# A hybrid DeltaNet and neighbourhood-attention layer on one core: transposes issued thirteen steps later, output-projection loads ahead of the network's, one more product between the token halves

## The chip, the cores and the metric

The kernel runs on one core of a Trainium2 chip. The metric is the device time of one execution in microseconds (us), as the median of repeated runs. A profile of one execution goes with it: its span runs from the first instruction to the last, and every instruction, wait and transfer in it has a place on that axis. Places such as "at 266 us" below are on that axis.

## The reference

One layer acts on 1024 latent tokens of width 1024, with 256 context tokens beside them. All arithmetic is in 32-bit floating point.

```python
px = modulate(rms_norm(x, norm1_w[i]), sh1, sc1) @ w_in[i]
pc = modulate(rms_norm(ctx, norm1_w[i]), csh1, csc1) @ w_in[i]
dn_c, s_ctx_f, s_ctx_b = gated_deltanet(pc[..., :DN_IN], ...)      # 4 heads of 128, forward and backward scan
dn_x, _, _ = gated_deltanet(px[..., :DN_IN], ..., s_ctx_f, s_ctx_b)
na_x = neighborhood_attention(qx, kx, vx, kc, vc, na_rpb[i], rows) # 8 heads of 64
x = x + g1 * (jnp.concatenate([dn_x, na_x], axis=-1) @ w_out[i])
x = x + g2 * swiglu(modulate(rms_norm(x, norm2_w[i]), sh2, sc2), w_ffn_in[i], w_ffn_out[i])
```

The delta rule is computed in chunks. Each chunk needs the inverse of a unit triangular matrix of its keys. The feed-forward network (`swiglu`) multiplies by a 1024 x 5632 matrix (gate and up halves) and then by a 2816 x 1024 matrix.

## The kernel before, in words

**How products are made.** Every large operand is split into a rounded upper part and a remainder (`whi`/`wlo`, `uhi`/`ulo` for weights, `hh`/`hl`, `hB`/`lB`, `hT`/`lT` for activations). ACT makes the upper part with a cast, DVE or POOL the lower part with a subtraction, and PE runs three products: upper by upper, upper by lower, lower by upper. So one 128 x 128 block of weights against 512 tokens is three matmuls of 128x512.

**The input projection (to about 550 us).** A list `jobs` of weight blocks is worked through in order: two key blocks first, then keys, the value columns, the attention's keys and queries, the DeltaNet's queries, values and gates. A job over the latent tokens has eight steps (one for each 128 rows of the input width) with six matmuls of 512 columns each. Background work is written as generators, and a call of `bg.step(n)` after each step takes it on by `n` `yield`s: one to a step before the job numbered `turn` (14), two on the ten pieces of a `Wide` job, three to a step from `turn` on. The background queue holds `block_inverses` and behind it `preps`. It starts with job 5.

`block_inverses` makes the decay tables, puts 32 x 32 blocks into a layout `N` of 80 partitions with PE transposes (L902-905), inverts them with 30 rounds of two DVE operations (L913, L915), writes the diagonal (L918, a memset), and takes them back with 32 PE transposes into PSUM and eight ACT copies into `WK` (L921-926). Then come for each scan direction a DVE transpose (L932), a store to `x_d` (L934), a DVE product (L935) and another store (L937). `preps` follows: for each chunk it loads `kk`, `xc` (from `x_d`) and `e`, copies blocks on ACT and POOL, takes exponentials on ACT, multiplies on DVE (`kk`, L981) and runs small matmuls into a bank `pr`, with ACT (L991) and DVE (L999) copies between them. The four context chunks come first; the sixteen latent ones wait until the DeltaNet's queries are done (end of job 18). A generator of `preps` has seven steps for each chunk, three chunks in turn.

**The output projection (about 780 to 877 us).** `two_blocks` has begun the first two of eight output blocks on the attention half of the rows. After the scans, `up = Stream()` issues the first eight loads (256 KB each) of the network's weights (`wq`, L1382) on the SP queue. Then come the remaining halves of the weights of blocks 0 and 1 (`wraw`, L215, two buffers), two loads of `x`, and while block 0 finishes, the load of block 2's weights. Blocks 2 to 5 take all tokens at a time; from block 2 on PSUM banks come from a pool `psf`, opened when the pool of the scans is closed. The last two blocks are run by token half `t`. After each half, `finish(t)` adds the two blocks to `x2` (L1454), squares them on ACT (L1459) and sums the squares in `acc` (L1460), and `normed(t)` multiplies `acc` by ones on PE and takes logarithm and exponential on ACT into `rs` (L1443-1445).

**The network's first two blocks, `PLAIN = 2` (about 877 to 928 us).** `x2` is cut into four quadrants: `B11`, `B21` (rows of the width, first token half) and `B12`, `B22` (second half). `quadrant` turns each of its four slices into network input: scale on DVE (L1541), bias on ACT (L1542), cast on ACT (L1534), remainder on DVE (L1535). Eight calls of `product` of 24 matmuls each follow: for block `f`, half `t`, row half `i`. `up.next()` hands out split weights (six buffers), `up.ahead` makes more. `sums` (L1553) prepares combined quadrants T1 to T4 for the blocks that follow, which use a seven-product scheme of Strassen's kind. From there on the network runs to the end.

**Who sets the order.** Each engine and the SP queue run their instructions in a fixed order. It is made when the program is built: the framework goes through the code in order, holds ready instructions by priority of that order, and places each by a model of how long everything takes, so that an instruction can come ahead of an earlier one that the model thinks is not ready. `tc.keep_in_program_order` pins an instruction to the code's order among those that are pinned on its engine. A pool opened with `reuse_waits="tile"`, as `pools` does, waits for the tiles that held its memory before; a pool opened without it waits for the whole pool.

Of the kernel before, what the change touches and what calls it, by code (L numbers as in the profile page):

```python
# [9 lines left out]
F32 = mybir.dt.float32  # L10
# [20 lines left out]
PLAIN = 2  # L31
SEGS = [(0, 256), (256, 512), (768, 512)]
# [55 lines left out]
def hybrid(ctx, tc, a, dbg):  # L88
# [304 lines left out]
    with ExitStack() as bs:  # L393
# [459 lines left out]
        def block_inverses():  # L853
            with ExitStack() as gs:
# [64 lines left out]
                yield  # L919
# [527 lines left out]
    with ExitStack() as os_:  # L1447
# [3 lines left out]

        def add(b, s, p):

            dve.scalar_tensor_tensor(x2[:, b, s], p, modp[:, 16 + b:17 + b], x2[:, b, s], op0=OP.mult, op1=OP.add)  # L1454
# [3 lines left out]
            sq = uw.tile([128, 4, 128], F32, name="ws", tag="ws", bufs=3).rearrange("p a b -> p (a b)")  # L1458
            act.activation(sq, x2[:, b, s], AF.Square)  # L1459
            dve.tensor_tensor(acc[:, s], acc[:, s], sq, OP.add)  # L1460
# [3 lines left out]
        for b, (w, outs) in enumerate(zip(ws, begun)):  # L1464
# [37 lines left out]
        for t, s in enumerate(HV):  # L1502
            outs = [bank(), bank()]
            last.append(outs)
            for k in range(KT):
# [4 lines left out]
                if t == 1 and k == 2:  # L1510
                    normed(0)
            if t == 0:
                finish(0)
# [5 lines left out]
    with ExitStack() as us:  # L1519
# [16 lines left out]

        def quadrant(n):
            i, j = int(n[1]) - 1, int(n[2]) - 1
            for k in range(4):
                kk, t = 4 * i + k, B[n][:, k]  # L1540
                dve.scalar_tensor_tensor(t, t, w2s[:, kk:kk + 1], rs[:, HV[j]], op0=OP.mult, op1=OP.mult)  # L1541
                act.activation(t, t, AF.Identity, bias=modp[:, 24 + kk:25 + kk])  # L1542
                split(X[n], B[n], k)
# [38 lines left out]
        quadrant("B11")  # L1582
        finish(1)
        quadrant("B21")
        prev = out_tiles(0)
        for f in range(PLAIN):
            po = [[bank(), bank()] for _ in range(2)]
            g = prev[f]
            w = [up.next(), None]
            for t in range(2):  # L1590
                for i in range(2):
                    if f == 0 and t == 1 and i == 0:
                        for n in ("B12", "B22"):
                            quadrant(n)
                    if t == 0 and i == 1:
# [187 lines left out]
```

## Time and profile before

| | |
|---|---|
| median of 3 runs | 1526.71 us (1526.71 to 1532.21) |
| the profiled execution | 1526.16 us |
| its span | 1524.4 us, mean granted clock 0.992 |
| PE busy | 1460.5 us (96%) |
| DVE, ACT, POOL busy | 66%, 47%, 12% of the span |
| share of the 16 DMA engines taken by the SP queue | 55.7%, 274 MB |

A row of the timeline gives start, duration, engine, line, operation, output and inputs, shapes and count of merged instructions, and in brackets how long the engine had been idle before and what ended that. PEld is the load of weights, which overlaps PE. SPq rows are the issue of transfers. A row of the windows gives the stretch, its length, the busy time of PE, PEld, DVE, ACT and POOL with the count of instructions, the granted clock of PE as a share of full speed, the share of the DMA engines and GB/s. A row of the waits gives who waited for whom, the total in us, how many times, and the longest.

### The profile page before, as it was taken

What the parts mean: (1) busy time and instruction counts of PE and PEld (TensorE: products, weight loads), DVE (VectorE), ACT (ScalarE), POOL (GpSimd) and SP (SyncE); (2) the same over time, 40 slices, a digit from 0 to 9 for tenths busy, and PEclk for the clock granted to TensorE, in tenths of its full rate; (3) what the DMA queues carried; (4) which work ended last, traced back from release to release, by engine and by line L of the source; (5) the groups of instructions that cost most, each with busy time, mean ns of one, the idle gap of its engine ahead of it and who ended that gap; (6) DMA issues with size and microseconds to landing.
All of it is one profiled execution on the core that took longest, in us unless ns stands there. A gap on an engine that the chain in (4) does not pass through costs nothing.

```text
span 1524.4 us, 23483 instructions
## 1 busy us (share of the span) xinstructions
PE 1460.5 (96%) x8365; PEld 1206.5 (79%) x8365; DVE 1004.4 (66%) x1898; ACT 710.6 (47%) x1387; POOL 184.8 (12%) x253
## 2 busy tenths in 40 slices
PE   5999998999999999998899989999999999999998
PEld 3789787778877778887787878888888888888887
DVE  4787579354677427779986388765655556599642
ACT  5443362683366546566642374333333334354441
POOL 0154610342134300000100000000000000000000
PEclk9999999899999999999999999999999999999999
DMA  9377223654477789998539315333233335798742
GB/s 367 112 229 238 61 78 122 234 152 168 132 217 253 223 280 278 285 273 237 164 102 330 109 35 186 111 104 104 104 104 103 104 104 173 246 364 294 235 152 83
DMA packets 209830, 276.29 MB, mean 181 GB/s; under 512 B 15968, under 2 KB 116912, under 8 KB 208688
## 3 DMA queue, kind: packets, MB, share of 16 engines
q1 hardware_dynamic: 208992, 274.41, 55.7%
q8 instruction: 66, 1.08, 0.3%
q14 instruction: 52, 0.43, 0.1%
q10 hardware_dynamic: 720, 0.37, 0.1%
HBM read 209.93 MB, written 68.98 MB: 183 GB/s over the span
## 4 chain that ended last, share of the span: by engine, by line
PE 75%; DVE 11%; DMA 4%; issue 4%; ACT 4%; POOL 1%; SPq 0%; POOLq 0%; DVEq 0%; ACTq 0%
PE ps L98 50%; PE blk L98 12%; PE sc L98 4%; PE pr L98 3%; PE m L98 3%; PE sc L102 2%; DVE tt L913 2%; DVE N L915 2%; DVE cacc L471 1%; PE m L102 1%; PE pm L98 1%; ACT bt L340 1%; DVE bt L337 1%; DMA wad<-wa 1%; DMA wraw<-w_out 1%
## 5 line engine op out<-in xcount | busy, mean ns | idle before, releaser
L98 PE MATMUL ps<-hT,uhi 128*128 128x512 f32 x496 | 147.1, 391 | 3.1 <-ACT hT L1534 3.1
L98 PE MATMUL ps<-lT,uhi 128*128 128x512 f32 x496 | 146.3, 389 | 0.0
L98 PE MATMUL ps<-hT,ulo 128*128 128x512 f32 x496 | 146.2, 389 | 0.0
L98 PE MATMUL blk<-hh,whi 128*128 128x512 f32 (+1 forms) x456 | 139.5, 398 | 2.2 <-ACT hh L714 1.5
L98 PE MATMUL ps<-hB,uhi 128*128 128x512 f32 x436 | 129.7, 391 | 0.0
L98 PE MATMUL ps<-lB,uhi 128*128 128x512 f32 x436 | 129.3, 390 | 0.0
L98 PE MATMUL blk<-hh,wlo 128*128 128x512 f32 (+1 forms) x456 | 129.1, 377 | 0.0
L98 PE MATMUL ps<-hB,ulo 128*128 128x512 f32 x436 | 128.9, 389 | 0.0
L98 PE MATMUL blk<-hl,whi 128*128 128x512 f32 (+1 forms) x456 | 128.7, 376 | 0.0
L1410 ACT CAST uhi<-ws 128x512 fp32r<-128x512 f32 x91 | 54.8, 623 | 153.0 <-PE ps L98 87.6
L1410 ACT CAST uhi<-wq 128x512 fp32r<-128x512 f32 x101 | 60.6, 621 | 135.3 <-PE ps L98 73.4
L98 PEld LDWEIGHTS ps<-hT,uhi 128*128 128x128 f32 x496 | 93.1, 188 | 22.7 <-ACT hT L1534 3.5
L1411 DVE TENSOR_TENSOR ulo<-wq,uhi 128x512 fp32r<-128x512 f32 x101 | 67.4, 688 | 66.0 <-ACT uhi L1410 37.6
L98 PEld LDWEIGHTS ps<-lT,uhi 128*128 128x128 f32 x496 | 93.3, 188 | 19.5
L98 PEld LDWEIGHTS ps<-hT,ulo 128*128 128x128 f32 x496 | 93.1, 188 | 19.3
L98 PEld LDWEIGHTS ps<-hB,uhi 128*128 128x128 f32 x436 | 82.1, 188 | 17.6 <-issue 0.5
L98 PEld LDWEIGHTS ps<-lB,uhi 128*128 128x128 f32 x436 | 82.1, 188 | 17.1
L98 PEld LDWEIGHTS ps<-hB,ulo 128*128 128x128 f32 x436 | 81.8, 188 | 17.0
L98 PEld LDWEIGHTS blk<-hh,wlo 128*128 128x128 f32 x456 | 80.5, 190 | 17.7 <-issue 2.5
L98 PEld LDWEIGHTS blk<-hl,whi 128*128 128x128 f32 x456 | 81.0, 190 | 15.7
L98 PEld LDWEIGHTS blk<-hh,whi 128*128 128x128 f32 x456 | 77.6, 193 | 18.9 <-ACT hh L714 3.1
L337 DVE CUSTOM_DVE_ANT_0 bt<-sc,bt 128x640 f32<-128x640 f32 x64 | 52.5, 822 | 49.1 <-issue 39.4
(332 smaller groups left out, 3057.9 us busy)
## 6 DMA issues: line engine op xcount, KB each, us to landing
wq<-w_fo SPq DMA_DIRECT2D x99, 256.0 KB
wq<-w_gu SPq DMA_DIRECT2D x88, 256.0 KB
wad<-wa SPq DMA_DIRECT2D x64, 256.0 KB
bt<-rpb SPq DMA_DIRECT2D x64, 192.0 KB
t_d<-g SPq DMA_DIRECT2D x22, 512.0 KB
fr<-t_d SPq DMA_DIRECT2D x44, 256.0 KB
f_d<-g SPq DMA_DIRECT2D x33, 256.0 KB
fr<-f_d SPq DMA_DIRECT2D x33, 256.0 KB
```

What stands on the lines that cost most here:

```text
L98: i = nc.tensor.matmul(*args, **kw)
L102: i = nc.tensor.transpose(*args, **kw)
L337: dve.tensor_tensor_reduce(bt, sc[:, u * 640:u * 640 + 640], bt, 1.0, -3.0e38, OP.add, OP.max, m[:, 0:1])
L340: act.activation(bt, bt, AF.Exp, bias=m[:, 1:2], accum_out=m[:, 2:3])
L471: dve.scalar_tensor_tensor(acc[:, d0:d1], p[:, d0 + o - s0:d1 + o - s0], cw[:, blk, tap:tap + 1], acc[:, d0:d1], op0=OP.mult, op1=OP.add)
L913: dve.tensor_tensor(t, N[:P, :, 0:c, c:c + 1].to_broadcast([P, 4, c, w]), N[:P, :, c:c + 1, c + 1:32].to_broadcast([P, 4, c, w]), OP.mult)
L915: dve.tensor_tensor(N[:P, :, 0:c, c + 1:32], N[:P, :, 0:c, c + 1:32], t, OP.add)
L1410: act.copy(hi, self.raw[key])
L1411: dve.tensor_tensor(lo, self.raw[key], hi.bitcast(F32), OP.subtract)
```

## The change

1. After the memset that ends the inversion, the generator yields thirteen times instead of once before it issues the transposes out of the layout.
2. `up = Stream()`, with its eight loads, stands behind the load of block 2's weights instead of ahead of the output projection. The pool `psf` is opened through `pools`, so with `reuse_waits="tile"`.
3. `normed(0)` is issued four matmuls earlier. `finish` is cut in two, and the DVE instructions of `finish`, and for `B11` and `B21` the scaling and the remainders, are pinned in an order written out by hand; the ACT ones are not.
4. The eight products come in the order `(f, t, i)` = 000, 001, **100**, 010, 011, **101**, 110, 111 instead of 000, 001, 010, 011, 100, 101, 110, 111. `B12` and `B22` are prepared behind the third product in the code.

```diff
+PRODUCTS = ((0, 0, 0), (0, 0, 1), (1, 0, 0), (0, 1, 0), (0, 1, 1), (1, 0, 1), (1, 1, 0), (1, 1, 1))
...
                 dve.memset(flat[:P, :, 0:1024:33], 1.0)
-                yield
+                for _ in range(13):
+                    yield
...
-    up = Stream()
-
     def finish(t):
 
+        sqs = []
         for b, o in zip((KT - 2, KT - 1), last[t]):
-            add(b, HV[t], o)
+            held(add_x(b, HV[t], o))
+            sqs.append(square(b, HV[t]))
+        if t:
+            yield
+        for sq in sqs:
+            held(dve.tensor_tensor(acc[:, HV[t]], acc[:, HV[t]], sq, OP.add))
...
             if b == 0:
                 nxt = load_w(a["w_out"][2], lo_engine=dve)
+                up = Stream()
         scopes.close()
-        ps = ctx.enter_context(tc.tile_pool(name="psf", bufs=8, space=PSUM))
+        ps = pools(ctx, "psf", bufs=8, space=PSUM)
...
-                if t == 1 and k == 2:
-                    normed(0)
+                    if t == 1 and k == 2 and j == 0:
+                        normed(0)
...
-        quadrant("B11")
-        finish(1)
-        quadrant("B21")
+        end = finish(1)
+        for k in range(4):
+            held(scaled("B11", k))
+            upper("B11", k)
+        for k in range(2):
+            held(lower("B11", k))
+        held(scaled("B21", 0))
+        held(lower("B11", 2))
+        next(end)
+        upper("B21", 0)
+        held(lower("B11", 3))
+        held(scaled("B21", 1))
+        for _ in end:
+            pass
+        upper("B21", 1)
+        held(lower("B21", 0))
+        for k in range(2, 4):
+            held(scaled("B21", k))
+            upper("B21", k)
+        for k in range(1, 4):
+            held(lower("B21", k))
         prev = out_tiles(0)
-        for f in range(PLAIN):
...
+        po, ws = {}, {}
+        for n, (f, t, i) in enumerate(PRODUCTS):
+            if n == 3:
+                for q in ("B12", "B22"):
+                    quadrant(q)
+            if (f, i) not in ws:
+                ws[f, i] = up.next()
+            if (f, t) not in po:
+                po[f, t] = [bank(), bank()]
+            product(po[f, t], ws[f, i], X[f"B{i + 1}{t + 1}"], i == 0)
+            if n == 0:
+                normed(1)
+            up.ahead(4 if n != 2 else 2)
+            if n >= 4:
+                for _ in range(4):
+                    next(todo, 0)
+            if i == 1:
+                g = prev[f]
+                act.activation(g[:, t], po[f, t][0], AF.Silu)
+                dve.tensor_tensor(g[:, t], po[f, t][1], g[:, t], OP.mult)
```

`scaled`, `upper` and `lower` are the three parts of `quadrant` as functions of their own (L1541; L1542 and L1534; L1535), `add_x` and `square` the two parts of `add` (L1454; L1459).

More of the change, by code (lines that the diff above doesn't have):

```diff
@@ L1457, in add @@
                 return
-            sq = uw.tile([128, 4, 128], F32, name="ws", tag="ws", bufs=3).rearrange("p a b -> p (a b)")
-            act.activation(sq, x2[:, b, s], AF.Square)
-            dve.tensor_tensor(acc[:, s], acc[:, s], sq, OP.add)
+            dve.tensor_tensor(acc[:, s], acc[:, s], square(b, s), OP.add)
         for b in range(2):
```

52 lines of the change are left out of this document (24 added, 28 removed).

## The prediction, before the result was known

> **What bounds the kernel now.** I read the page first (busy shares and the chain that ended last), then the list of waits of PE, then the granted clock and busy time in windows around each wait, and last the timeline on both sides of the waits that the change touches.
>
> ```profile
> PE 1460.5 (96%) x8365; PEld 1206.5 (79%) x8365; DVE 1004.4 (66%) x1898; ACT 710.6 (47%) x1387; POOL 184.8 (12%) x253
> ```
>
> PE is busy for 1460.5 of the 1524.4 us span, so what can be won without removing matmuls is the rest, 64 us, and the time that PE runs slowly. PE's waits (total, count, longest) in 255-300, and then in 775-960:
>
> ```profile
> PE m L102 <- DVE N L918: 5.4, 1, 5.4
> PE pr L98 <- DVE kk L981: 1.9, 1, 1.9
> ```
>
> ```profile
> PE ps L98 <- ACT hT L1534: 3.1, 1, 3.1
> PE sc L98 <- ACT whi L216: 2.1, 1, 2.1
> PE ps L98 <- ACT ws L1459: 1.7, 1, 1.7
> PE ps L98 <- DVE acc L1460: 0.8, 1, 0.8
> ```
>
> All but the second stand where the diff edits: the wait for the inverses (5.4), for block 1's split weights (2.1), at the pool change (1.7), for the sums of squares (0.8) and for the cast of B12 (3.1), 13.1 us together. The windows show what each costs beyond its own length. The columns after the length are PE, PEld, DVE, ACT and POOL busy; the decimal behind POOL is the granted clock, then DMA share and GB/s.
>
> ```profile
> 260.90:266.50 5.60, 0.21 (x1) 0.00 (x0) 5.26 (x11) 0.00 (x0) 0.00 (x0) 0.87 0.26 102
> 266.50:275.30 8.80, 8.78 (x42) 7.68 (x43) 1.63 (x4) 3.41 (x8) 0.00 (x0) 0.50 0.43 150
> 293.40:295.30 1.90, 0.03 (x1) 0.03 (x1) 0.69 (x1) 1.81 (x7) 0.84 (x3) 1.00 1.00 347
> 296.00:300.00 4.00, 4.00 (x24) 3.09 (x24) 0.61 (x2) 3.62 (x7) 0.81 (x3) 0.60 0.85 236
> 799.70:801.90 2.20, 0.06 (x1) 0.00 (x0) 0.02 (x2) 0.62 (x1) 0.00 (x0) 1.00 1.03 392
> 801.90:804.00 2.10, 2.09 (x9) 1.75 (x10) 2.06 (x3) 0.60 (x1) 0.00 (x0) 1.00 1.08 353
> 890.30:893.60 3.30, 0.23 (x2) 0.00 (x0) 2.67 (x5) 2.48 (x4) 0.00 (x0) 0.92 0.00 0
> 893.60:897.60 4.00, 3.95 (x12) 3.15 (x13) 4.00 (x8) 3.97 (x7) 0.00 (x0) 0.64 0.13 50
> 900.00:940.00 40.00, 40.00 (x178) 33.10 (x177) 37.36 (x61) 22.05 (x41) 0.00 (x0) 1.00 0.31 102
> ```
>
> PE stands still from 260.9 to 266.5 and then runs 8.8 us at half clock. The stop at 890.3 is followed by 4 us at 0.64, the one at 293.4 by 4 us at 0.60, and the one at 799.7 by none. In 900-940 PE starts 178 matmuls in 40 us, 0.225 us each, so a step of six matmuls is 1.35 us and a product of 24 is 5.4 us.
>
> **Part one: the transposes.** Nothing is removed or added. The 32 transposes, eight ACT copies, two DVE transposes and two DVE products, four stores on SP, and then all of `preps` (loads on SP, copies on POOL and ACT) are issued twelve steps later. The rows of the chain:
>
> ```profile
> 266.52 0.53 PE L102 MATMUL m<-cst,N 80*128 80x80 f32 x2 [5.41 <-DVE N L918]
> ...
> 267.05 0.28 DVE L915 TENSOR_TENSOR N<-N,tt 80x120 f32<-80x120 f32 x1
> ...
> 295.27 1.62 PE L98 MATMUL pr<-fx,kk 128*128 128x96 f32 x8 [1.90 <-DVE kk L981]
> ```
>
> By the code, 6 + 1 + 8 + 3 + 4 + 30 + 1 = 53 yields lie ahead of the transposes now and 65 then. Jobs 5 to 7 give 24 background steps, the `Wide` job 20, each job after it eight, so they are issued at step 54 in job 10 now and at step 66 in job 11 then. At one step of 1.35 us that is 16.2 us more matmuls ahead of them, so PE reaches them at 260.9 + 16.2 = 277.1 or later, and DVE's last write of `N` is at 267.3. The cover is ten us; four of the twelve steps would already do. The wait of 5.4 goes, and with it the half clock behind it: 8.8 us at 0.50 holds 4.4 us of full-speed work, so 4.4 more. Together 9.8.
>
> What is late next is the chain behind the transposes. From the first transpose to the first `pr` matmul PE's own work was 295.3 - 1.9 - 266.5 = 26.9 us, of which 4.4 by the half clock: 22.5 at full clock. The chain of copies, stores, loads and the DVE product took 28.8 us. Its first part is the transposes themselves, which also ran at half clock, so it shortens by between nothing and 4 us. If the same matmuls lie between, the wait before `pr` is between 28.8 - 4 - 22.5 = 2.3 and 6.3 us where it was 1.9. The other end is that it vanishes, with the 4 x 0.4 = 1.6 us of lost clock behind it: a gain of 3.5. The worst is 4.4 more wait and as much more half clock, 8.8 lost. I take 1.5 lost, near the short end, since the transposes fill most of the first 9 us of that chain. Part one: 9.8 - 1.5 = **8.3**.
>
> That context chunks now fall where `bg.step` takes three steps instead of one is no cost in itself while PE has other matmuls. The latent chunks start at step 205 in both, since they wait for job 18, and the context ones end by step 100 instead of 88, so the end of `preps` does not move.
>
> A rule to weigh: the Trainium skill, TensorE: Matmul & The Clock Gate, section Part 1: The HAM clock gate (the "warmup" mystery), says that PE's clock halves after an idle window of about 3.4 us and comes back after about as long of busy time. By that the loss behind the first stop would be 1.7 instead of 4.4, and a stop of 3.1 or 1.9 us need not cost any. The trace differs in length (8.8 us at 0.50) and in threshold (0.60 behind 1.9 us, 1.00 behind 2.2), and I go by the trace; by the page the sum would be about 4 us smaller.
>
> **Part two: the loads.** The eight loads are moved on SP past block 1's load, two loads of `x` and block 2's load.
>
> ```profile
> 769.41 0.61 SPq L215 DMA_DIRECT2D wraw<-w_out  x1
> 791.54 3.65 SPq L1382 DMA_DIRECT2D wq<-w_gu  x8
> 795.28 0.40 SPq L215 DMA_DIRECT2D wraw<-w_out  x1
> 795.78 0.94 SPq L1463 DMA_DIRECT2D x<-xcT  x2
> 797.07 0.56 SPq L215 DMA_DIRECT2D wraw<-w_out  x1
> ```
>
> And on the engines, the two casts that wait for these loads, and the last read of the old PSUM pool:
>
> ```profile
> 801.24 0.62 ACT L216 CAST whi<-wraw 128x512 fp32r<-128x512 f32 x1 [2.26 <-DMA wraw<-w_out]
> ...
> 805.60 1.05 ACT L216 CAST whi<-wraw 128x1024 fp32r<-128x1024 f32 x1 [0.91 <-DMA wraw<-w_out]
> ...
> 807.83 1.40 DVE L1454 SCALAR_TENSOR_TENSOR x<-sc,modp,x 128x512 f32<-128x512 f32 x2
> ```
>
> SP stands from 770.0 until 791.5, when the memory of `wq` comes free, and block 1's load stands behind it. It needs only a second `wraw` buffer. Issued by 791.5 instead of 795.3 and not behind 2 MB, with the same six us to land (795.3 to 801.2), it is there by 797.5, and PE asks for it at 799.7. The 2.1 go. At the pool change, PE waited until L1454 had read the last old bank (807.83 + 1.40 = 809.2); tile by tile, `psf` can start on banks that the scans left long before. Then block 2's weights are next. PE asked for them at 809.2 - 1.7 = 807.5, and will at 805.4. If they land no earlier than now, their cast ends at 805.6 + 1.05 = 806.65, PE waits 1.2 where it waited 1.7, and only 0.5 is gained; if the load is 3 us earlier, all goes. Between 0 and 3.8, I take **3.5**. What falls behind is the network's weights, which PE needs only after six more output blocks. The loads after block 2 have two `wraw` buffers that come free earlier than now; if that failed, block 3 would wait instead.
>
> **Part three: the network's first products.**
>
> ```profile
> 890.92 3.40 DVE L1541 SCALAR_TENSOR_TENSOR x<-x,w2s,rs 128x512 f32<-128x512 f32 x5 [2.76 <-ACT rs L1445]
> ...
> 893.00 0.60 ACT L1534 CAST hT<-x 128x512 fp32r<-128x512 f32 x1
> ...
> 905.56 0.69 DVE L1535 TENSOR_TENSOR lB<-x,hB 128x512 fp32r<-128x512 f32 x1
> ```
>
> Two remainders fewer stand ahead of the sums of squares on DVE (0.69 each, as in the last row), and `normed(0)` comes four matmuls, 0.9 us, earlier; so `acc` is ready about 2 us sooner and the 0.8 goes. The pinned additions of `finish(1)` are DVE instructions that wait for the projection's last matmul; behind them on DVE stand B11's last remainder and B21's scaling, which PE needs later than that. The products of B11 and B21 then end at 889.5 instead of 890.3, the extra product fills PE until 894.9, and the first cast of B12 ended at 893.6 with `rs` as late as now. So the 3.1 go with a margin of 1.3, and with them the slow clock: twelve matmuls started in 893.6-897.6 where 4.0 / 0.225 = 18 fit, 1.3 us. The sum is 0.8 + 3.1 + 1.3 = 5.2. Next is B22: PE comes to its product at 900.3 and to its last remainder 4.5 us on, at 904.8; that was written at 906.25 and will be about 0.9 earlier, 905.35. I subtract 0.5: **4.7**, with 0 and 5.4 as ends.
>
> A new wait: the six weight buffers. Block 1's weights for the lower row half get a buffer only when the product 010 is done, and are needed one product later instead of three. Casts of them on ACT stand ahead of casts of B22 and T1, for which PE waits; a cast and a remainder take 1.3 us and the product between takes 5.4, so I cost it at nothing. If that cover were gone it would be up to 2.6.
>
> **Sum.** 8.3 + 3.5 + 4.7 = 16.5. The profiled execution took 1526.16, so 1509.7; the median of the runs is 0.55 above that execution: **1510**.
>
> **Rivals.** *The wait moves from the transposes to `pr`.* Part one then keeps 9.8 - 8.8 = 1.0, and the time is 1526.7 - 1.0 - 3.5 - 4.7 = 1517.5. For it: the chain of 28.8 us does not go by PE's clock. Against: it needs the worst end at each point. 0.12.
>
> *The loads gain nothing*, because the DMA engines are full either way (1.03 and 1.08 in the windows): 1513.7. The Trainium skill, DMA: Bandwidth & Descriptors, section Queues, rings and completion order, says that descriptors on an engine are consumed in ring order, which speaks for an earlier landing; no row here separates the two. 0.08.
>
> *DVE takes over in the network.* It is busy 37.36 of 40 us in 900-940, and PE now comes 5 us sooner. Part three then gives 0: 1515. Against: from `rs` to the product that reads T4, PE has twelve products, 65 us, to run. 0.08.
>
> *The order does not come out as written*, because the program's order is made by a model at build time, and the product 100 or the loads are put back: 1526. 0.05.
>
> *Slower: the context chunks stall PE.* Of their 28 generator steps, 16 now run three to a matmul step, and about nine of these hold `pr` matmuls. If each stops PE as the one at 293.4 did (1.9 and 1.6 of clock, 3.5), that is 31.5, and the time 1526.7 - 16.5 + 31.5 = 1541.7. It decides from five such stops on. Against it stands that the latent chunks, four times as many, run at that pace already, with these waits of PE in 420-530:
>
> ```profile
> PE pr L98 <- ACT kk L991: 2.5, 1, 2.5
> PE pr L98 <- DVE y L999: 1.5, 3, 0.8
> ```
>
> It gets 0.05.
>
> **The numbers.** The forecast has 0.62. 0.5% is 7.6 us, about what a measurement here can tell from no change; faster means below 1519. The forecast, the second and third rivals and most of the first lie there: 0.85. The fourth and a remnant of the first make 0.10, the last 0.05. Low end: all gains at their best, 9.8 + 3.5 + 3.8 + 5.4 = 22.5, 1504. High end: the first rival, 1518.
>
> **What would show it.** Right: no wait on L918 and full clock where the transposes run; no wait of `sc` on L216 and of `ps` on L1459; no wait on `hT`, full clock through the first eight products. Wrong: a wait before `pr` over 4 us with half clock behind it; block 2 or 3 waiting on `whi`; PE waiting on `lB` or `uhi` in the network's first 50 us. The prediction as a whole fails if PE's idle time in the three places together falls by less than 7 us.

## The result and the profile after

The change makes the kernel 0.3% slower: 1532.42 us against 1529.16 us, medians of 20 runs each, ratio 1.003 with a 95% interval of 1.002 to 1.0041. The prediction was 1510, in a range from 1504 to 1518.

The first line of the page after stands against the first line shown of before: PE is busy for the same matmuls 3.5 us longer, and idle for 4 us more.

```profile
PE 1464.0 (96%) x8365; PEld 1208.2 (79%) x8365; DVE 1007.2 (66%) x1898; ACT 715.2 (47%) x1391; POOL 185.9 (12%) x253
```

PE's waits after, in 255-360 and then in 775-1010 (line numbers are one to seven higher than before):

```profile
PE m L103 <- ACT cr L521: 6.2, 2, 5.9
PE m L103 <- ACT WK L928: 3.9, 1, 3.9
PE pr L99 <- DVE kk L983: 2.6, 1, 2.6
...
PE ps L99 <- DVE x L1461: 4.0, 1, 4.0
PE ps L99 <- DVE e L1702: 1.5, 1, 1.5
```

Every wait that the prediction wanted gone is gone: `N` (5.4), `whi` (2.1), `ws` (1.7), `acc` (0.8), `hT` (3.1). In their place stand two rows of waits on ACT at the transposes (6.2 and 3.9), one on `add(1)` (4.0) and one in the network (1.5). In the windows after, behind the length, PE's busy time and clock show the price at the new waits and behind them:

```profile
275.00:281.00 6.00, 0.21 (x1) 0.00 (x0) 0.00 (x0) 3.75 (x6) 2.34 (x1) 0.70 0.08 23
281.00:297.00 16.00, 12.05 (x45) 9.04 (x46) 3.04 (x2) 11.85 (x18) 2.37 (x1) 0.58 0.29 74
...
813.00:818.20 5.20, 1.21 (x7) 0.67 (x5) 5.03 (x9) 4.20 (x9) 0.00 (x0) 0.86 1.04 395
818.20:823.00 4.80, 4.80 (x11) 3.76 (x12) 4.27 (x7) 0.56 (x1) 0.00 (x0) 0.50 0.94 281
```

Where the time went is read from the start of the same instruction in both traces (after less before): -1.5 at 166-256, ahead of the change; +5.5 at 416-552; +8.3 at 562-780; +11.1 at 820; +8.0 from 1004 to the end. So part one costs 7.0, part two 2.4, part three wins 3.1, and 2.8 fall between 552 and 562, where nothing was changed. That last stretch counts as chance: over the seventeen traces of the other runs that change nothing there it differs by 0 to 4 us. The two profiled executions lie 7.8 apart, the medians 3.3.

Why ACT is late at the transposes is read from the timeline after, ACT and then SP:

```profile
277.22 1.04 ACT L217 CAST whi<-wraw 128x1024 fp32r<-128x1024 f32 x1 [20.41 <-DMA wraw<-w_nqk]
278.17 1.08 ACT L463 ACTIVATE cacc<-blk 128x512 f32<-128x512 f32 x2
279.26 1.28 ACT L521 ACT_TABLE_LOAD   x1
280.56 1.05 ACT L521 ACTIVATE cr<-m,bias 128x256 f32<-128x256 f32 x2
...
288.50 0.75 ACT L928 COPY WK<-m 128x320 f32<-128x320 f32 x2
```

```profile
251.28 11.60 SPq L1060 DMA_DIRECT2D vw_d<-nv_d  x6
262.97 4.38 SPq L216 DMA_DIRECT2D wraw<-w_nqk  x1
```

Twelve steps on, the transposes stand behind the norm of block 3's attention keys, which holds both `m` banks from 265 us. ACT empties them at 280.56, behind the cast of the next job's weights, for which it had been idle 20.41 us. The first copies into `WK` come behind the rest of that norm, at 288.50, and end the second wait. The load of the weights was issued at 262.97, behind sixteen copies of `nv_d` into `vw_d` (256 KB each, made ready for the attention), and the share and rate of the DMA engines (last two columns) show what they do to it:

```profile
262.00:268.00 6.00, 6.00 (x24) 4.30 (x23) 3.50 (x9) 0.00 (x0) 0.00 (x0) 1.00 0.26 102
268.00:272.00 4.00, 4.00 (x19) 3.31 (x18) 0.00 (x0) 0.00 (x0) 0.00 (x0) 1.00 0.61 205
272.00:277.00 5.00, 3.21 (x15) 2.32 (x13) 0.00 (x0) 0.00 (x0) 0.00 (x0) 1.00 0.25 89
```

A share of 0.26 is about that of four engines of sixteen (0.25). SP took 4.38 us to issue the load, where it took 0.60 for the same load in a_held below, and none of the load's pieces moved before 268. Three quarters of them moved by 272; the last quarter, which by the share lies behind the copies on the four engines, moved up to 277. The cast came as late in the kernel before, at 278.83 behind an idle time of 4.43 us, but there the eight copies into `WK` (268.72 to 274.40) were ahead of it on ACT, so it held up nothing of PE. The trace of before had it, and a row that the prediction quotes for the clock (260.9 to 266.5) ends in "0.26 102".

### The profile page after: what moved, and what is told of

Read it like the earlier page. It is cut to its first block, busy times and chain, and to the rows that moved or that the text cites. A ratio compares the mean times of both kernels' runs of the same rounds, so it can differ in the third digit from the quotient of the medians.

```text
span 1532.1 us, 23478 instructions
## 1 busy us (share of the span) xinstructions
PE 1464.0 (96%) x8365; PEld 1208.2 (79%) x8365; DVE 1007.2 (66%) x1898; ACT 715.2 (47%) x1391; POOL 185.9 (12%) x253
## 4 chain that ended last, share of the span: by engine, by line
PE 71%; DVE 10%; DMA 8%; ACT 6%; issue 2%; POOL 1%; SPq 1%; POOLq 0%; DVEq 0%; ACTq 0%
PE ps L99 45%; PE blk L99 13%; PE sc L99 4%; PE m L99 3%; PE pr L99 3%; PE sc L103 2%; DMA nv_d<-zt 2%; DVE cacc L472 1%; DMA wad<-wa 1%; DMA wraw<-w_nqk 1%; DVE cacc L492 1%; DVE acc L253 1%; DMA bt<-rpb 1%; PE pm L99 1%; PE m L103 1%
## 5 line engine op out<-in xcount | busy, mean ns | idle before, releaser
L99 PEld LDWEIGHTS ps<-hT,uhi 128*128 128x128 f32 x496 | 93.0, 188 | 21.3 <-ACT uhi L1412 1.9
```

The lines of the kernel that those rows point to most:

```text
L99: i = nc.tensor.matmul(*args, **kw)
```

## The experiments

The theory: the moved transposes are made to wait by the late weights, over cast, norm, banks and copies. Its rivals: the move costs at any place; or the stall only passes on to the next chain. "Lost" is PE's idle time plus its busy time by the missing share of the clock, summed over windows of 5 us. (The expectations call PE TensorE, and so on.)

| run | median, us | ratio to before, 95% | lost 240-360 | lost 360-420 |
|---|---|---|---|---|
| before | 1526.71 to 1529.16 | 1 | 13.4 | 0 |
| after | 1532.42 | 1.003 (1.002 to 1.0041) | 20.1 | 0 |
| a_only | 1534.91 | 1.0047 (1.003 to 1.0065) | 22.1 | 0 |
| a_spread | 1537.90 | 1.0062 (1.0038 to 1.0086) | 23.6 | 0 |
| a_y4 | 1534.73 | 1.0038 (1.0018 to 1.0058) | 19.0 | 0 |
| a_y4_dve | 1533.42 | 1.0035 (1.0017 to 1.0053) | 19.8 | 0 |
| late_only | 1527.75 | 1.0011 (0.9994 to 1.0029) | 14.2 | 0 |
| a_late | 1534.53 | 1.0046 (1.0029 to 1.0062) | 18.6 | 0 |
| a_y6_late | 1539.76 | 1.0087 (1.0065 to 1.0109) | 22.5 | 0 |
| held_only | 1544.37 | 1.0101 (1.0082 to 1.012) | 12.2 | 17.0 |
| a_held | 1543.36 | 1.0096 (1.0072 to 1.0121) | 5.3 | 20.3 |
| a_y10_held | 1542.13 | 1.0084 (1.0067 to 1.0102) | 10.3 | 21.3 |
| slow_only | 1545.73 | 1.0115 (1.0092 to 1.0138) | 20.3 | 0 |
| a_slow | 1545.61 | 1.0111 (1.0089 to 1.0132) | 4.8 | 12.6 |
| fin | 1554.96 | 1.0169 (1.0144 to 1.0193) | 6.8 | 0.8 |
| b_only | 1529.07 | 1.0003 (0.9988 to 1.0018) | 12.3 | 0 |
| b_late | 1529.36 | 1.0002 (0.9986 to 1.0018) | 17.5 | 0 |
| b_psf | 1528.22 | 0.9993 (0.9977 to 1.0009) | 14.0 | 0 |
| c_only | 1525.33 | 0.9974 (0.9959 to 0.9989) | 13.2 | 0 |
| c_psf | 1524.85 | 0.9974 (0.9957 to 0.999) | 13.7 | 0 |

Each sum is from one execution. In 240-360 seven traces with nothing changed up to there (before, late_only and the five of the other two parts) lie between 12.3 and 17.5, and three with the thirteen yields and the copies in their old place (a_only, a_late, after) between 18.6 and 22.1; so some 5 us between two of these sums can be chance.

### Each part alone

**a_only** is the kernel before with the thirteen yields.

```diff
-                yield
+                for _ in range(13):
+                    yield
```

> The thirteen yields alone; the rest is the kernel before. Theory: the transposes now come behind the norm of block 3's keys and behind the cast of the next job's weights on ScalarE, whose load lands late, so two waits (about 5.9 us at the transposes' product and 3.9 us at the second group of copies, with half clock between them) take the place of the one of 5.4 us: +5 to +7 us, 1.004 to 1.005 of before, and the wait before the row of pr stays near 2.6 us. Rival one, the prediction's sum for this part: the wait of 5.4 us goes and nothing takes its place, -8.3 us (0.995). Rival two, the offset seen after 550 us belongs to the later parts or to chance: within 2 us of before.

The medians differ by 7.3 us. PE's waits in 255-360 are those of after (6.6, 3.9, 3.1). The first rival, the prediction's sum for this part, is out, and so is the second, that this part costs nothing.

**b_only** is the kernel before with the second part:

```diff
-    up = Stream()
...
                 nxt = load_w(a["w_out"][2], lo_engine=dve)
+                up = Stream()
...
-        ps = ctx.enter_context(tc.tile_pool(name="psf", bufs=8, space=PSUM))
+        ps = pools(ctx, "psf", bufs=8, space=PSUM)
```

> The loads' order and the tile-wise reuse of the network's first PSUM banks alone. Theory: out-projection's wait for block 1's weights goes (2.2 us), but w_out's third load and its casts now stand ahead of the second half of add(1) on VectorE, the bank it frees comes late by 4 us, and the network's first loads come later: +1 to +3 us (1.001 to 1.002), with a wait of about 4 us that the multiply-add of add(1) ends. Rival, the prediction's sum for this part: -3.5 us (0.998).

No difference that can be measured: the gain that was counted on is not there, nor, clear of chance, the loss of 1 to 3 us that was expected. The wait of 2.1 us on `whi` is gone, and this one has come, in 770-850:

```profile
PE ps L98 <- DVE x L1452: 4.5, 1, 4.5
```

**c_only** is the changed kernel with parts one and two undone (the diffs above, backwards).

> The order of the products, the split finish, the held quadrants alone, with one yield and the old order of loads. Theory: the wait at the second token half's first product (3.1 us) and at the sum of squares (0.8 us) and the slow clock behind them go, 5.2 us, of which 2.1 to 2.6 us are given back where VectorE frees PSUM banks late behind the modulation's accumulations: -2.5 to -3.5 us (0.998). Rival, the prediction's sum for this part, with nothing given back: -4.7 us (0.997). Rival two, the gain is tied to the other two parts: within 1 us.

By the ratio it wins 4 us (1.7 to 6.3), by the medians 2.2. The waits on `hT` and `acc` are gone, and this one is new, in 860-1010:

```profile
PE ps L99 <- DVE e L1702: 1.7, 1, 1.7
```

The three ratios together give 1.0024, and the whole change measured 1.003: the parts add up, and part one is what went wrong.

### Is it the late weights?

**a_spread** adds to a_only a copy with another outermost dimension:

```diff
-                    sp.dma_start(vw_d[:, cb, ch], vlat[4 * ch:4 * ch + 4, BLKS[cb]:BLKS[cb] + 32])
+                    sp.dma_start(vw_d[:, cb, ch].rearrange("(r c) d -> c r d", r=4),
+                                 vlat[4 * ch:4 * ch + 4, BLKS[cb]:BLKS[cb] + 32].rearrange("r c d -> c r d"))
```

> The thirteen yields, and the copies of nv_d into vw_d with 32 instead of 4 in their outermost dimension, the same bytes. Theory: as they stand these copies hold 4 of the 16 DMA engines (DMA share 0.26 over some 25 us), a quarter of the next job's weights waits behind them, the cast of these on ScalarE waits for that quarter and the transposes' copies wait behind the cast. Spread, the load lands some 5 us earlier and the first wait (5.9 us) shrinks to under 2 us: 5 to 9 us faster than the yields alone (0.998 to 1.001 of before). Rival: ScalarE's place in the norm of block 3's keys, not the load, ends the wait; then the copies' spread changes nothing against the yields alone (1.004 to 1.005). Rival two: 2,048 byte pieces over all engines get in the way of more loads, slower than the yields alone.

The waits at the transposes fell from a_only's 10.5 to 3.4 us as the theory has it, and the time did not. With other transfers the framework made another order: SP now stood 24.1 us in front of a store of the norm and the next load behind it came late. PE's waits in 255-360:

```profile
PE blk L98 <- ACT whi L216: 5.2, 1, 5.2
PE pr L98 <- DVE y L1000: 4.5, 1, 4.5
PE pr L98 <- DVE kk L982: 2.6, 1, 2.6
PE m L98 <- ACT WK L927: 2.1, 2, 1.6
PE m L102 <- ACT cr L520: 1.3, 1, 1.3
```

Two things were changed at once, so this run settles nothing; it puts up the rival that the stall passes on.

**a_y4** and **a_y4_dve** ask for a better place: `range(4)` in place of `range(13)`, and in the second also

```diff
-                    act.copy(U[:, :, i0:i0 + 4], p[:, :4 * P].rearrange("p (i u) -> p u i", i=4))
+                    dve.tensor_copy(U[:, :, i0:i0 + 4], p[:, :4 * P].rearrange("p (i u) -> p u i", i=4))
```

> Four yields in place of thirteen, alone: the transposes three steps on instead of twelve, so that they and the first six of their eight copies still stand ahead of the next weights' cast on ScalarE, and the last two copies behind it. Three steps are 4.1 us of products on TensorE by the before profile (18 products from 261 us on). Theory (what hurts is the place behind that cast, not the moving): the wait of 5.4 us falls to about 1.3 us, and TensorE stops instead ahead of the norm of block 3's keys, whose banks wait for the last two copies behind the cast at 278 us: some 3 to 5 us there; -3 to +1 us in all (0.998 to 1.0005), at any rate 5 us or more faster than thirteen yields. Rival, the prediction's way of counting: the 4.1 us are simply won, with half of the slow clock behind them, -5 to -7 us (0.996). Rival two, moved transposes cost whatever their place: +5 us.

> Four yields, and the eight copies out of the transposes' banks on VectorE, which was busy 0.7 us of 265 to 275 us, in place of ScalarE. Then no copy stands behind the weights' cast. Theory: the wait of 5.4 us falls to about 1.3 us, no new one ahead of the norm, -4 to -7 us against before (0.995 to 0.997) and 3 to 5 us faster than four yields with the copies on ScalarE. Rival: the norm waits for the cast through its own sum of squares in any case, so that the copies' engine changes nothing: as with ScalarE. Rival two: VectorE's copies push back its work for the norm, the wait comes back before the row of pr: 0 to -2 us.

Both theories missed: for a_y4 -3 to +1 us were expected and 5.8 came (by the ratio), which is the figure of its second rival, a cost at any place. The times of these two runs don't speak against that rival; a_held and fin below do. Four yields moved the transposes by five matmuls only, 1.1 us, not by three groups, so the first wait kept 4.2 of its 5.4 us. In a_y4 the norm then waited on the last copies, as the theory said, though 2.5 us and not 3 to 5. With the copies on DVE that wait is absent, but PE waits 6.0 us at the row of `pr`: on DVE the second `ut` (290.39) stands behind the work of the norm, which waits for the late cast on ACT.

**late_only**, **a_late** and **a_y6_late** were to issue the copies seven jobs later, with one, thirteen and six yields:

```diff
-            if isinstance(j, Wide) and n == values:
+            if n == values + 7:
                 copies.add(windows())
```

> The kernel before, with the sixteen copies of nv_d into vw_d issued seven jobs later; every engine's order but SyncE's is that of before. Control for the next run. In the before run the weights that land at 278 us behind these copies hold up ScalarE only after the transposes' copies, and nothing of TensorE. Theory: the load lands near 270 us, TensorE's waits of 5.4 and 1.9 us stay, within 1.5 us of before (0.999 to 1.001). Rival: the late load costs before too, through the norm's place on ScalarE and VectorE ahead of the first preps: -2 to -4 us. Rival two: the copies get in the way where they now are: +1 to +3 us.

> Thirteen yields, and the sixteen copies seven jobs later; every engine's order but SyncE's is that of the thirteen yields alone, so that only the time changes at which the next weights land. Theory (the late weights on the path cast, norm, banks, copies make the new waits): they land near 270 us, the wait of 6.2 us at the transposes shrinks to under 1.5 us and that of 3.9 us at the second group to under 2 us; idle and slow clock of TensorE from 240 to 420 us, 22.1 us with the yields alone and 13.4 before, fall to 12 to 16 us, and the time to -2 to +2 us of before (0.999 to 1.001), 5 us or more faster than the yields alone. Rival one (what the spread copies suggested: the stall goes on to the next load, cast and norm, whatever is removed): the first wait shrinks, others of the same sum come, and the time stays at +5 us or more (1.003 to 1.006). Rival two, the prediction's: with nothing in the way, -6 to -8 us (0.995).

> Six yields in place of thirteen, and the copies seven jobs later. In the program's order the first transposes then stand 5 to 6 groups of products behind their old place and still two groups ahead of the end of their job, two of the eight copies ahead of the next weights' cast and the others behind it and the norm. Theory: with the weights landing early, the cast holds nothing up; the wait of 5.4 us falls under 1.5 us, the norm's banks cost at most 2 us, the row of pr keeps its 1.9 us: -3 to -6 us against before (0.996 to 0.998). Rival, the conserved stall: the sum of idle and slow clock from 240 to 420 us stays at 18 us or more, +3 to +6 us.

The copies did not move. In late_only's timeline of SP they stand where they stood, since the framework puts a transfer that nothing pins where its model has it ready:

```profile
251.13 11.60 SPq L1058 DMA_DIRECT2D vw_d<-nv_d  x6
262.83 4.38 SPq L215 DMA_DIRECT2D wraw<-w_nqk  x1
```

In the first two SP's and PE's orders are those of before and of a_only from end to end. So they are repeats of these kernels, and agree with them (1.0011 and 1.0046). The third is six yields alone, 13 us behind before by the ratio, more than any of its expectations. It has the first wait down to 1.5 us and pays at the norm, because two of its eight copies are ahead of the late cast (278.64) and six behind it:

```profile
PE m L98 <- ACT WK L927: 7.4, 1, 7.4
PE pr L98 <- ACT kk L992: 6.5, 2, 5.0
...
PE m L102 <- DVE N L918: 1.5, 1, 1.5
```

**held_only** and **a_held** pin the copies in the program's order, beside the later place; PE's order stays that of before and of a_only from end to end, and in a_held those of ACT and DVE stay a_only's up to 350.

```diff
-                    sp.dma_start(vw_d[:, cb, ch], vlat[4 * ch:4 * ch + 4, BLKS[cb]:BLKS[cb] + 32])
+                    tc.keep_in_program_order(sp.dma_start(vw_d[:, cb, ch], vlat[4 * ch:4 * ch + 4, BLKS[cb]:BLKS[cb] + 32]))
```

> The kernel before, with the sixteen copies of nv_d into vw_d held in the program's order, seven jobs later. TensorE's, ScalarE's and VectorE's orders are those of before. Control for the next run. Theory: the next weights land near 268 us and not at 278; the wait of 5.4 us stays, since VectorE's inverses set it: within 2 us of before (0.999 to 1.001). Rival: the late weights cost before too, by the norm ahead of the first preps on ScalarE and VectorE; then the wait of 1.9 us at the row of pr goes and 2 to 4 us with it (0.997 to 0.999).

> Thirteen yields, and the same copies held seven jobs later; TensorE's and ScalarE's orders are those of the thirteen yields alone, so that only the time changes at which the next weights land. Theory (the late weights on the path cast, norm, banks, copies): they land near 270 us, the wait of 6 us at the transposes shrinks to under 1.5 us, that of 3.9 us at the second group to under 2 us; idle and slow clock of TensorE from 240 to 420 us, 22.1 us with the yields alone, fall to 12 to 16 us, and the time is 5 us or more below that of the yields alone (0.998 to 1.001). Rival one (the stall passes on): the first wait shrinks, others of the same sum come further on, the time stays at +5 us or more (1.003 to 1.006). Rival two, the prediction's: with nothing in the way -6 to -8 us (0.995).

This is the run that tells. In a_held SP issues the load in 0.60 us, the cast comes at 268.65 and waits for PE to be done with its buffer, not for the load. The two rows, and then PE's waits in 255-360:

```profile
261.47 0.60 SPq L215 DMA_DIRECT2D wraw<-w_nqk  x1
268.65 1.05 ACT L216 CAST whi<-wraw 128x1024 fp32r<-128x1024 f32 x1 [7.67 <-PE blk L98]
```

```profile
PE pr L98 <- DVE kk L982: 2.2, 1, 2.2
PE pr L98 <- DVE y L1000: 0.8, 1, 0.8
PE m L102 <- ACT cr L520: 0.7, 2, 0.4
```

Of 6.6 and 3.9 us at the transposes 0.7 are left, with the same order on PE, ACT and DVE. The stretch 240-360 loses 5.3 us against 12.2 in its control: with the weights early the yields win 6.9 us there. No trace without the yields goes under 12.2 in this stretch, and the three that have all thirteen with the weights early (a_held, a_slow, fin) lie between 4.8 and 6.8. But both kernels lose 17 and 20 us in 360-420, where the held copies stand in one row ahead of the next weights (SP issues six of them from 359.47 to 375.28 in held_only, PE then waits 14.2 us), and the times are alike. Both were expected near before and are some 15 us behind it, and their times show nothing of the yields' gain.

**a_y10_held** is a_held with ten yields.

> Ten yields, and the copies held seven jobs later. Here the norm of block 3's keys stands whole ahead of the transposes on ScalarE and all eight copies ahead of the next cast. Theory: with the weights early, neither cast nor norm holds the banks when the transposes come; the wait of 5.4 us goes, what is left is under 3 us up to the row of pr, -3 to -7 us against before (0.995 to 0.998). Rival, the stall passes on: the copies and the norm's chain of some 10 us on ScalarE with its table loads make TensorE wait 5 us or more somewhere from 270 to 345 us, +3 us or more (1.002 to 1.006).

The rival is nearer: 10.3 us lost up to 360, with 3.3 at `pr` and 1.9 at `m`. By this stretch thirteen is the better place once the weights are early; the times of the two do not differ.

**slow_only** and **a_slow** issue the pinned copies two to a job over eight jobs:

```diff
-            if isinstance(j, Wide) and n == values:
+            if n == values + 5:
                 copies.add(windows())
...
-                    copies.step(2)
+                    copies.step(k in (1, 2))
```

> The kernel before, with the sixteen copies held in the program's order and issued two to a job over eight jobs, from the fifth job after. TensorE's and ScalarE's orders up to the transposes' end are those of before. Control for the next run. Theory: two copies hold a quarter of a load's pieces some 5 us, less than the job of 12 us or more by which it comes early: no hole like that of 14 us; the wait of 5.4 us stays; within 3 us of before (0.999 to 1.002). Rival: the copies hold up the preps' fetches and stores on SyncE: +4 us or more (1.003 or more).

> The same, with the thirteen yields. Theory: as in the run with the held copies, no wait over 1 us at the transposes; idle and slow clock of TensorE from 240 to 360 us 5 to 7 us, against 12 to 14 in the control, and the time 5 to 8 us below that of the control (0.995 to 0.997 of it), what the prediction gave for this part. Rival one (the stall passes on): the time is that of the control within 2 us. Rival two (yields cost in themselves): 5 us above the control.

Up to 360 a_slow loses 4.8 us, its control 20.3; then a_slow waits 11.1 us at 370, and from 417 to 560 both run level. The control was expected within 3 us of before and is 17 us behind it, as its rival said. For the time of a_slow the first rival has it right. What stopped a_slow was a fetch of `preps` for which ACT waited 10.56 us: SP came to the next weights only at 366.74, issued two copies behind them and then the fetch, at 369.22, and it took 9 us to land (ACT went on at 378.40). So in both places that were tried for the copies something further on was late, and its price hid the yields' gain. That the copies alone made this fetch late is not shown.

**fin** does without the copies: the attention fetches its windows from `nv_d` itself. It holds the yields, the third part and the tile-wise banks, not the moved loads.

```diff
-            sp.dma_start(vw, vw_d[:, cb, half:half + 3, hp * 128:hp * 128 + 128])
+            for r in range(4):
+                sp.dma_start(vw[32 * r:32 * r + 32],
+                             nv_d[CT:].rearrange("(q r c) d -> r c q d", r=4, c=64)
+                             [r, BLKS[cb]:BLKS[cb] + 32, half:half + 3, hp * 128:hp * 128 + 128])
...
-            if isinstance(j, Wide) and n == values:
-                copies.add(windows())
```

> The whole change without the moved loads of part two (the tile-wise banks stay), and without the copies: each fetch of a window of values is four loads of 32 partitions out of nv_d in place of one out of vw_d. TensorE's and ScalarE's orders at the transposes are those of the thirteen yields. Theory (late weights made the new waits, the copies the holes further on): no wait over 1 us at the transposes, idle and slow clock of TensorE 5 to 7 us from 240 to 360 us (13.4 before, 20 with the change) and under 3 us from 360 to 420 us; 6 to 9 us there and 2 to 4 us by the products' order: -8 to -12 us against before (0.992 to 0.995), if the 128 small loads stay hidden in the attention. Rival one (the stall passes on by another load or store): 360 to 420 us lose 5 us or more, the time is that of the third part alone (0.997 to 0.999). Rival two: the small loads are late for the attention, its stretch from 550 to 800 us is 5 us or more longer, 1.000 or more.

The mechanism came out as the theory has it and the time as its second rival. Up to 548 the orders of PE, ACT and DVE are those of a_only. Windows of a_only and then of fin, 240-300, 300-360 and 360-420:

```profile
240.00:300.00 60.00, 49.42 (x218) 38.41 (x216) 28.47 (x32) 21.66 (x32) 7.63 (x3) 0.86 0.33 105
300.00:360.00 60.00, 56.12 (x302) 42.68 (x302) 32.25 (x37) 44.00 (x86) 24.71 (x39) 0.94 0.62 196
360.00:420.00 60.00, 60.00 (x354) 52.44 (x352) 34.56 (x46) 26.61 (x42) 14.64 (x15) 1.00 0.51 153
```

```profile
240.00:300.00 60.00, 59.30 (x274) 46.88 (x273) 36.10 (x38) 30.12 (x42) 11.57 (x8) 1.00 0.25 73
300.00:360.00 60.00, 56.79 (x325) 44.41 (x324) 34.31 (x39) 45.88 (x94) 29.87 (x46) 0.94 0.74 226
360.00:420.00 60.00, 59.23 (x378) 51.20 (x377) 38.89 (x55) 22.83 (x40) 9.45 (x6) 1.00 0.50 157
```

PE idles 0.7 instead of 10.6 us in 240-300, at full clock, and gives nothing back up to 551. Measured on the same instructions, fin is 1.6 us ahead of before at 256 and 6.6 at 551: the yields with the weights early win 5 us where alone they lost 7. Up to 360, ahead of their holes, a_held wins 6.8 in the same way and a_slow 7.3. Some of fin's gain may be the copies' absence; in held_only, without yields, it was worth 1.2 up to 360, less than two repeats differ. In 560-820, where the 128 small loads take the place of 32, all is lost: fin goes from 6.6 us ahead to 32 behind. That the loads did this was the second rival's forecast; no run takes them apart from the new order of the attention that came with them.

### The loads and the banks

**b_late** creates `up` behind `add(1)`, just ahead of the new pool, instead of behind block 2's load; **b_psf** has the tile-wise banks alone (last diff line of b_only).

> The network's first loads and casts one block later still, behind add(1), with the tile-wise reuse of the banks; the rest is the kernel before. In the change's place five of the six lower halves stand on VectorE ahead of add(1)'s second pair; here one does. Theory: these casts hold add(1) and with it the second PSUM bank: the wait of 4.5 us at the third block's second product falls under 2 us, the wait on the weights of block 1 stays away: -2 to -4 us against the change's order alone, -1 to -3 us against before (0.998 to 0.9995). Rival: the bank comes late for another reason (the sums of the modulation, which now stand ahead of add(1)): the wait stays at 3 us or more, and the time that of the change's order (1.000).

> The tile-wise reuse of the network's PSUM banks alone, loads as in the kernel before. Theory: of the wait of 1.7 us ahead of the third block's first product, which the squares of block 1 end, up to 1.3 us goes and nothing else changes: -1.5 to 0 us (0.999 to 1.000), and the wait on block 1's weights (2.1 us) stays. Rival: the wait moves to the second product, which needs the bank that add(1) frees last: no change.

In b_late the wait fell from 4.5 to 3.7 only. The lower halves are away from ahead of `add(1)`, and the sums of the modulation have taken their place on DVE (809.04 to 812.72, with one lower half among them), as the rival said. In b_psf the wait before the pool change turned into one at the second product, which needs the bank that `add(1)` frees: the rival again. In 770-850:

```profile
PE ps L98 <- DVE x L1452: 3.7, 1, 3.7
```

```profile
PE sc L98 <- ACT whi L216: 1.5, 1, 1.5
PE ps L98 <- DVE x L1454: 1.4, 1, 1.4
```

**c_psf** is c_only with the tile-wise banks.

> The order of the products with its finish (the change's third part) and the tile-wise banks, without the moved loads and without the yields. Theory: the parts add up, -2.2 to -4 us of the third part and 0 to -1.5 us of the banks: -2.5 to -5 us against before (0.9967 to 0.9984). Rival: the banks' reuse shifts the third part's gain away: within 1 us of before.

It comes in as expected, at 0.9974, the same ratio as c_only. These two are the fastest, 4 us under before by the ratio; no version was found that keeps the yields and beats before.

## Why the prediction was wrong, step by step

**Part one, the first term: "The wait of 5.4 goes, and with it the half clock behind it".** It went, and "PE reaches them at 277.1" was close: in fin the transposes start at 274.97 on an axis that runs 1.6 us ahead. The step that failed is the next one, "What is late next is the chain behind the transposes": only the way from the transposes on to `pr` was followed, not what they need to start. They need a bank of `m` and a place on ACT, and twelve steps on both belong to a norm that stands behind a cast that waits for a load. -8.3 was forecast, +7.3 measured, which is most of what separates 1510 from 1532. That the missing piece was the load's lateness is shown by a_held against held_only (6.9 us won up to 360) and by fin; that the cover itself was there ("the cover is ten us") is shown by the same runs. "Four of the twelve steps would already do" is not borne out: with three steps (a_y4) the transposes moved by 1.1 us and 4.2 of the 5.4 stayed, with five (a_y6_late) 1.5 stayed. And "Nothing is removed or added" holds for the code alone: in their new order ACT's instructions need four table loads more (41 against 37, 1.28 us each), though none of PE's new waits ends on one of the four.

**The wait before `pr`.** 2.3 to 6.3 was given; 2.6 measured, and the first rival, which needs more than 8 us there, is out. But the working behind the range did not hold. It says "if the same matmuls lie between": from the first transpose to the first `pr` matmul PE started 113 matmuls before and 150 after, and the way took 43.9 us (36.2 in a_held), not 28.8. Both sides of the difference grew, so the number is right by luck.

**Part two.** The first step, "Issued by 791.5 instead of 795.3", came close. At this place the axis after runs 8.7 us behind that of before, and a time is compared only when that is taken off. SP got the second load's buffer at 801.65, which is 793 on the axis of before, and the cast followed 2.9 us later, where it took 6.0 behind the eight loads of the network. The wait on `whi` went.

```profile
778.62 23.41 SPq L216 DMA_DIRECT2D wraw<-w_out  x2
804.52 0.62 ACT L217 CAST whi<-wraw 128x512 fp32r<-128x512 f32 x1 [2.09 <-DMA wraw<-w_out]
```

What failed is the step at the pool change. "`psf` can start on banks that the scans left long before" held for the first product only; the second takes the bank that `add(1)` frees, and that addition now stands behind five lower halves of the network's weights. DVE after:

```profile
813.43 1.29 DVE L1413 TENSOR_TENSOR ulo<-wq,uhi 128x512 fp32r<-128x512 f32 x2
814.89 1.90 DVE L1413 TENSOR_TENSOR ulo<-wq,uhi 128x512 fp32r<-128x512 f32 x3 [0.17 <-ACT uhi L1412]
816.70 1.40 DVE L1461 SCALAR_TENSOR_TENSOR x<-sc,modp,x 128x512 f32<-128x512 f32 x2
```

The prediction followed eight loads and not the casts that come with them. On the same instructions the wait on `whi` is worth 2.4 us and the new one costs 4.8. -3.5 was forecast; b_only measured +0.5, with an interval from -1.8 to +2.7.

**Part three.** The 0.8, the 3.1 and the 1.3 went as worked out: on the same instructions each of the four traces that hold this part (after, c_only, c_psf, fin) wins 5.2 us between 880 and 960, the sum to the tenth. B22 did not wait. What was given back came 70 us on: PE, now earlier, waits 1.5 to 2.5 us for PSUM that DVE frees behind sums of the modulation, and in c_only runs at a clock of 0.94 in 960-975. With the slow clock that takes back 2.1 (after) to 4.6 us (fin). That is the third rival's engine, at a place that the prediction did not look at. -4.7 was forecast, 2.2 (medians) to 4 (ratio) measured in c_only: right in kind, a little large.

**The slower rival** had the wrong place: the context chunks cost nothing that shows but one wait of 0.8 us. The test that the prediction set itself, PE's idle time in the three places falling by 7 us or more, came out the other way: the waits listed were 15.0 us before and are 18.2 after.

**The rule on transfers.** The prediction cited ring order for part two, where no row of before could separate its rival, "The loads gain nothing". The runs bear it out: block 1's load took 6.0 us to its cast behind the network's loads and 2.9 ahead of them, and at the transposes the load is late behind the copies and not without them. The same page of the Trainium skill, DMA: Bandwidth & Descriptors, section Why a DMA increments its semaphore by 16 and not by 1, says that a transfer is split over as many engines, up to sixteen, as divide the outermost sizes of both its sides. The traces agree: an outermost size of 4 gave a share of 0.26, and the copies with 32 in a_spread gave 0.69, of which this is the row:

```profile
240.00:250.00 10.00, 10.00 (x53) 8.49 (x52) 9.69 (x10) 0.00 (x0) 0.00 (x0) 1.00 0.69 220
```

## What to carry to other kernels

When work is moved behind other work, list what it needs to start there, bank by bank and queue by queue, and who holds each at that place; the wait that it leaves tells nothing of this. A transfer that lands late without harm is a debt: look in the trace for casts that waited long for a load though nobody waited for them. And a later line in the code moves an instruction only if the framework's order follows; the timeline has to show that the edit happened before its time is read.

## What the runs showed of the hardware

- Sixteen copies of 256 KB from memory to memory with an outermost size of 4 moved 102 GB/s at a share of 0.26, and each of the last six kept SP for 1.9 us (11.60 for six). A load behind them kept SP for 4.38 us instead of 0.60, and its last quarter moved up to 277, 14 us after its issue (262.97).
- Behind a stop of 5.9 us, with one of 3.9 us within the stretch, PE ran at 0.58 for 16 us (281 to 297); behind one of 4.0 us at 0.50 for 4.8 us (818.2 to 823). Much shorter stops went either way: behind one of 1.66 us in c_only PE ran at 0.69 for 4.1 us (956.9 to 961), behind one of 1.47 us in after at 1.00 (968 to 975).
- A copy of 128x320 from PSUM took 0.49 us on DVE (a_y4_dve) and 0.43 on ACT (before).
